# Five buffers for the upper and four for the lower halves of the expert weights in place of three each, and nine load buffers in place of twelve

## The chip, the cores and the metric

The kernel runs on one core of a Trainium2 chip. The metric is the device time of one launch in microseconds (us), the median of several executions. TensorE is called PE here, VectorE DVE, ScalarE ACT, SyncE SP, as in the profile; SP issues the transfers from memory.

## The reference

Two decoder layers over 256 tokens of width 1024, all in fp32. Nearly all of the time goes into the last step, the routed experts: a router picks two of eight experts for each token, and each expert is a SwiGLU of width 3584.

```
xt = rmsnorm(x) * (1 + scale) + shift                  # 256 x 1024
logits = xt @ w_router                                 # 8 experts
top_logits, top_idx = top_k(logits, 2); gates = softmax(top_logits)
y_e = (silu(x_e @ w_gate[e]) * (x_e @ w_up[e])) @ w_down[e]    # rows x_e routed to e
x = x + gate * sum over the chosen experts of gates * y_e
```

Ahead of it stand layer 0 (a retention mixer and a dense SwiGLU of width 2816) and layer 1's pooling mixer; behind it the last norm.

## The kernel before, in words

**Weights.** Every weight is read once, in parts of 128 x 2048 fp32 (1 MB). `load` (L126) takes a buffer from the deque `ring` and issues one transfer on SP's queue. That queue is in order: a load that waits for its buffer holds up all loads behind it. `weights` (L136) then splits the part: ACT writes the upper half `w_hi` (the value rounded to the matmul type fp32r), DVE the lower half `w_lo` = raw − `w_hi`, both at L113 in `split`. `w_hi` and `w_lo` have `N_SPL` = 3 buffers each, so the split of a part can begin once PE is through with the part three before it. The loads of the expert stage rotate over 12 lasting buffers: six `raw`, four `e8`, and the two old tiles `cb` and `T_l`, which are free by then (`SPARE`, L59, whose first number is the place in the deque).

**Matmuls.** A wide expert (ranks 1 to 3 by the number of tokens) takes three matmuls per 512 weight columns in `mm3` (L156 to L158: upper x upper, lower weight x upper, upper weight x lower token). A narrow one has the upper and lower halves of 64 tokens side by side and needs two, `mm2` (L738 with `w_hi`, L739 with `w_lo`).

**Blocks.** Each expert has seven blocks. A block has two parts of gate weights, two of up and two of down; the down parts come two blocks later. That makes 336 parts, numbered 0 to 335 in this document, from about 460 us to about 1358 us. The first seven blocks are those of a narrow expert; then blocks come in the order wide, narrow, wide, narrow, wide, narrow, narrow, repeated.

**Small work between the parts.** `g_out` and `u_out` (L766) take a narrow block's results out of the banks, L774 transposes and adds them, `sg` (L753) and `moe_h` (L755) do a wide block's. `behind_next` ties these evictions behind a split of the coming weights. Where an expert's tokens are gathered, `prepare` runs 32 small matmuls (L720), eight evictions `xe_f` on ACT (L240), and a split into `xe_n` (L113). Where an expert ends, `combine` scales two banks into `y_g` (DVE, L799), splits them into `yp` (L113), multiplies back (L809, L810) and adds into `xs` (DVE, L811). Eight blocks from the end `f_row` (ACT, L193) is made for the last norm.

**Order.** A scheduler fixes one static order on each engine when the program is built, from the code and the buffers. An instruction that waits holds up all behind it on its engine.

Of the kernel before, what the change touches and what calls it, by code (L numbers as in the profile page):

```python
# [11 lines left out]
R = mybir.dt.float32r  # L12
# [33 lines left out]
N_RAW, N_SPL, N_E8, N_OHT = 6, 3, 4, 4  # L46
# [9 lines left out]
assert len(set(BLOCKS)) == NE * NJ and BLOCKS[-1] == (NE - 1, NJ - 1)  # L56
ALWAYS = math.inf

SPARE = ((8, "a8", 2, 2), (11, "kd", 1, 3), (12, "qk", 1, 10), (12, "cb", 1, ALWAYS), (9, "T_l", 1, ALWAYS))  # L59

ADA_B, ADA_O, ADA_F = (1, 1, 1, 1, 1, 1, 1, 1), (3, 3, 0, 0), (0, 0, 4, 4, 3, 3, 3, 3, 3, 3, 0)

# [2 lines left out]
def trunk(ctx, tc, x, cols, c_row, const, ada_0, ada, w_0, w_in, w_out, f_gu, f_dn, pool_w, m_g, m_u, m_d, out):  # L65
# [13 lines left out]
    def buf(tag, shape, bufs=1, dt=F, name=None):  # L79
        return act.tile([P] + shape, dt, tag=tag, name=name or tag, bufs=bufs)  # L80
# [24 lines left out]
    cb = buf("cb", [2048])[:, :D]  # L105
# [6 lines left out]
    def split(hi, lo, src):  # L112
        return nc.scalar.activation(hi, src, AF.Copy), nc.vector.tensor_sub(lo, src, hi.bitcast(F))  # L113

    @contextmanager
    def behind(*instructions):

        with ExitStack() as s:
            for i in instructions:
                s.enter_context(tc.issue_after(i.ins))  # L120
            yield


    ring = deque([("raw", N_RAW, ALWAYS)] * N_RAW)

    def load(src, in_halves=False):  # L126
        tag, bufs, uses = ring.popleft()
        if uses > 1:
            ring.append((tag, bufs, uses - 1))
        t = buf(tag, [2048], bufs, name="raw")  # L130
        n = 1024 if in_halves else 2048
        for c in range(0, 2048, n):
            nc.sync.dma_start(t[:, c:c + n], src[:, c:c + n])
        return t

    def weights(src, step=2048, held=((), (), (), ()), in_halves=False):  # L136

        parts, splits = [], []
        for h in range(0, src.shape[1], 2048):
            t = load(src[:, h:h + 2048], in_halves)  # L140
            hi = buf("w_hi", [2048], N_SPL, R)
            lo = buf("w_lo", [2048], N_SPL, R)
            for c in range(0, 2048, step):
                strip = slice(c, c + step)
                with behind(*held[len(splits)]):
                    splits.append(split(hi[:, strip], lo[:, strip], t[:, strip]))
            parts.append((hi, lo))

        def at(c, n=512):
            hi, lo = parts[c // 2048]  # L150
            return hi[:, c % 2048:c % 2048 + n], lo[:, c % 2048:c % 2048 + n]
        at.splits = splits
        return at
# [119 lines left out]
    for k in range(KD):  # L273
        ada_sums(ada_0[k], (k, 8 + k), None if k else ada_first)
        nc.scalar.activation(mod[:, k:k + 1], mod[:, k:k + 1], AF.Identity, bias=col[:, C_ADAB + k:C_ADAB + k + 1])
        nc.vector.scalar_tensor_tensor(a1[:, k:k + 1], mod[:, 8 + k:9 + k], scale1[:, k:k + 1], gain_of(0, 0)[:, k:k + 1],
                                       op0=ALU.add, op1=ALU.mult)
        h_k = mod_T(hh[:, k], hl[:, k], xT[:, k], a1, mod, k)
        at = weights(w_0[k], 1024, held=((), h_k))
        for f in range(4):  # L280
            wh, wl = at(512 * f)
            for b in range(TB):
                mm3(first[f][b], hh[:, k, tok(b)], hl[:, k, tok(b)], wh, wl, k == 0, k == KD - 1)
    kd = buf("kd", [K_BAND - K_DM])
# [85 lines left out]
    for i, f in enumerate(W_REST):  # L370
        at = weights(w_in[i])
        pss = [bank() for _ in range(TB)]
        for k in range(KD):
            wh, wl = at(512 * k)
            for b in range(TB):
                mm3(pss[b], hh[:, k, tok(b)], hl[:, k, tok(b)], wh, wl, k == 0, k == KD - 1)
        win_done(f, pss, st)
        for fn, h in after.get(i, []):
            fn(h, st)
        ada_next(ADA_B[i])  # L380
    g_row = row(buf("g_row", [D]), mcol(0, 2))
    acc = [[bank() for _ in range(2)] for _ in range(TB)]
    for h in range(NH):
        yT = st[f"yT{h}"]
        at = weights(w_out[h])
        last = h == NH - 1
        steps = [(i, b) for i in range(4) for b in range(TB)]
        if last:
            steps = [(i, b) for b in range(TB) for i in range(4)]
        for i, b in steps:  # L390
            for n in range(2):
                wh, wl = at(1024 * i + 512 * n)
                mm3(acc[b][n], yT[:, 0, i, tok(b)], yT[:, 1, i, tok(b)], wh, wl, h == 0 and i == 0, last and i == 3)
        ada_next(ADA_O[h])
# [205 lines left out]
    srcs = sources()  # L600


    once = [ring[i][:2] + (1,) for i in range(2)]
    ring.rotate(-2)
    for place, *spare in SPARE:
        ring.insert(place, tuple(spare))
# [416 lines left out]
```

## Time and profile before

| | |
|---|---|
| Median of 3 runs | 1374.83 us (1373.33 to 1375.98) |
| The profiled execution | 1376.74 us, of which its span 1375.0 us |
| PE matmul, DVE, ACT busy | 96 %, 88 %, 71 % of the span |
| Mean granted TensorE clock | 0.991 |
| Moved from memory | 475 MB, 346 GB/s over the span |

The busy shares are averages over all stages. In the profile's groups a line such as L113 stands for every split, so the tile's name tells which one it is. An idle time in brackets is the engine's wait just before the row, with the instruction that released it. A row of PE is longer than the distance to the next row, since matmuls overlap.

### The profile page before, as it was taken

What the parts mean: (1) busy time and instruction counts of PE and PEld (TensorE: products, weight loads), DVE (VectorE), ACT (ScalarE), POOL (GpSimd) and SP (SyncE); (2) the same over time, 40 slices, a digit from 0 to 9 for tenths busy, and PEclk for the clock granted to TensorE, in tenths of its full rate; (3) what the DMA queues carried; (4) which work ended last, traced back from release to release, by engine and by line L of the source; (5) the groups of instructions that cost most, each with busy time, mean ns of one, the idle gap of its engine ahead of it and who ended that gap; (6) DMA issues with size and microseconds to landing.
All of it is one profiled execution on the core that took longest, in us unless ns stands there. A gap on an engine that the chain in (4) does not pass through costs nothing.

```text
span 1375.0 us, 16794 instructions
## 1 busy us (share of the span) xinstructions
PE 1315.1 (96%) x6136; PEld 1052.5 (77%) x6136; DVE 1215.2 (88%) x1121; ACT 978.2 (71%) x942; POOL 0.2 (0%) x4
## 2 busy tenths in 40 slices
PE   7999998999999899999999999999999999999995
PEld 5787876888887777778778877788778777777874
DVE  7889867998867698999989999989998989999997
ACT  6655465444445698878878887878878878788884
POOL 0000000000000000000000000000000000000000
PEclk9999999999999899999999999999999999999998
DMA  9987885998786599999999999999999999999960
GB/s 384 380 278 260 324 287 207 338 378 362 297 333 238 209 427 344 369 364 424 419 377 401 424 334 334 412 356 426 412 357 409 360 334 401 404 367 418 424 279 33
DMA packets 66474, 477.30 MB, mean 347 GB/s; under 512 B 7377, under 2 KB 7761, under 8 KB 8658
## 3 DMA queue, kind: packets, MB, share of 16 engines
q1 hardware_dynamic: 66386, 476.17, 88.3%
q8 instruction: 50, 0.82, 0.2%
q14 instruction: 38, 0.31, 0.1%
HBM read 475.10 MB, written 1.05 MB: 346 GB/s over the span
## 4 chain that ended last, share of the span: by engine, by line
PE 70%; DVE 16%; ACT 6%; issue 4%; DMA 3%; DVEq 0%; SPq 0%; ACTq 0%
PE bank L157 15%; PE bank L158 15%; PE bank L156 14%; DVE w_lo L113 12%; PE bank L739 8%; PE bank L738 7%; PE tbank L774 3%; ACT w_hi L113 3%; DMA raw<-in_m_d_dram 2%; PE tbank L720 2%; PE tbank L250 1%; DVE raw L167 1%; ACT xe_f L240 1%; DMA raw<-in_m_u_dram 1%; DVE dT L113 1%
## 5 line engine op out<-in xcount | busy, mean ns | idle before, releaser
L113 DVE TENSOR_TENSOR w_lo<-raw,w_hi 128x2048 fp32r<-128x2048 f32 (+1 forms) x413 | 907.1, 2225 | 82.5 <-ACT w_hi L113 78.4
L113 ACT ACTIVATE w_hi<-raw 128x2048 fp32r<-128x2048 f32 (+1 forms) x413 | 763.8, 1868 | 199.1 <-PE bank L158 142.3
L739 PE MATMUL bank<-w_lo,xe_n 128*128 128x512 f32 x560 | 230.7, 412 | 12.7 <-DVE w_lo L113 9.6
L738 PE MATMUL bank<-w_hi,xe_n 128*128 128x512 f32 x560 | 221.1, 396 | 2.0 <-DVE xe_n L113 2.0
L739 PEld LDWEIGHTS bank<-w_lo,xe_n 128*128 128x128 f32 x560 | 105.8, 189 | 57.5 <-DVE w_lo L113 38.0
L156 PE MATMUL bank<-w_hi,T_h 128*128 128x512 f32 x352 | 140.9, 401 | 3.0 <-ACT T_h L113 3.0
L157 PE MATMUL bank<-w_lo,T_h 128*128 128x512 f32 x352 | 138.5, 393 | 2.4 <-DVE w_lo L113 2.4
L158 PE MATMUL bank<-w_hi,T_l 128*128 128x512 f32 x352 | 138.8, 394 | 1.7 <-DVE T_l L113 1.7
L157 PE MATMUL bank<-w_lo,xe 128*128 128x512 f32 x336 | 132.5, 394 | 0.9 <-DVE w_lo L113 0.9
L156 PE MATMUL bank<-w_hi,xe 128*128 128x512 f32 x336 | 131.6, 392 | 0.0
L158 PE MATMUL bank<-w_hi,xe 128*128 128x512 f32 x336 | 130.9, 390 | 0.0
L738 PEld LDWEIGHTS bank<-w_hi,xe_n 128*128 128x128 f32 x560 | 106.0, 189 | 22.1 <-DVE xe_n L113 2.1
L167 DVE SCALAR_TENSOR_TENSOR raw<-raw,cb 128x1024 f32<-128x1024 f32 x96 | 114.4, 1218 | 1.7 <-DMA raw<-in_ada_dram 1.7
L739 PE MATMUL bank<-w_lo,dT 128*128 128x512 f32 x280 | 104.4, 411 | 7.2 <-DVE w_lo L113 6.7
L738 PE MATMUL bank<-w_hi,dT 128*128 128x512 f32 x280 | 100.1, 394 | 1.7 <-DVE dT L113 1.7
L157 PE MATMUL bank<-w_lo,dT 128*128 128x512 f32 x256 | 100.8, 394 | 0.7 <-DVE w_lo L113 0.7
L158 PE MATMUL bank<-w_hi,dT 128*128 128x512 f32 x256 | 99.8, 390 | 0.0
L156 PE MATMUL bank<-w_hi,dT 128*128 128x512 f32 x256 | 94.2, 389 | 0.0
L156 PEld LDWEIGHTS bank<-w_hi,T_h 128*128 128x128 f32 x352 | 66.6, 189 | 17.7 <-ACT T_h L113 4.3
L158 PEld LDWEIGHTS bank<-w_hi,T_l 128*128 128x128 f32 x352 | 66.5, 189 | 17.1 <-DVE T_l L113 3.2
L157 PEld LDWEIGHTS bank<-w_lo,T_h 128*128 128x128 f32 x352 | 66.6, 189 | 16.4 <-DVE w_lo L113 2.8
L157 PEld LDWEIGHTS bank<-w_lo,xe 128*128 128x128 f32 x336 | 63.1, 188 | 16.3 <-DVE w_lo L113 3.8
(227 smaller groups left out, 1430.5 us busy)
## 6 DMA issues: line engine op xcount, KB each, us to landing
raw<-in_m_g_dram SPq DMA_DIRECT2D x112, 1024.0 KB, 7.5
raw<-in_m_u_dram SPq DMA_DIRECT2D x112, 1024.0 KB, 7.6
raw<-in_m_d_dram SPq DMA_DIRECT2D x112, 1024.0 KB, 7.3
raw<-in_ada_dram SPq DMA_DIRECT2D x48, 1024.0 KB, 7.2
raw<-in_f_gu_dram SPq DMA_DIRECT2D x22, 1024.0 KB, 6.9
raw<-in_w_in_dram SPq DMA_DIRECT2D x16, 1024.0 KB, 5.2
raw<-in_f_dn_dram SPq DMA_DIRECT2D x11, 1024.0 KB, 7.2
raw<-in_w_dram SPq DMA_DIRECT2D x8, 1024.0 KB, 8.7
```

The source lines that it names most:

```text
L113: return nc.scalar.activation(hi, src, AF.Copy), nc.vector.tensor_sub(lo, src, hi.bitcast(F))
L156: nc.tensor.matmul(ps, xh, wh, start=start, stop=False)
L157: nc.tensor.matmul(ps, xh, wl, start=False, stop=False)
L158: nc.tensor.matmul(ps, xl, wh, start=False, stop=stop)
L167: nc.vector.scalar_tensor_tensor(s, s, 1.0, cb, op0=ALU.mult, op1=ALU.mult, accum_out=mod[:, m:m + 1])
L240: nc.scalar.activation(out, ps, AF.Identity, scale=a[:, k:k + 1], bias=s[:, k:k + 1])
L250: nc.tensor.transpose(ps[:, i * P:(i + 1) * P], src[:, i * P:(i + 1) * P], ident)
L720: nc.tensor.matmul(ps[:, i * ns:(i + 1) * ns], xn[:, b, c], oh[:, b, 0:ns], start=(b == 0), stop=(b == TB - 1))
L738: nc.tensor.matmul(ps, x, wh, start=start, stop=False)
L739: nc.tensor.matmul(ps, x, wl, start=False, stop=stop)
L774: nc.tensor.matmul(ps[:, i, c], a[:, c * P:(c + 1) * P], fold, start=True, stop=True)
```

## The change

Before the expert stage begins, two deques of split buffers grow. `uppers` gets the two old tiles `cb` and `T_l` beside the three `w_hi`, `lowers` one buffer of tag `e8` beside the three `w_lo`. `SPARE` loses its entries for `cb` and `T_l`, and `ring` one `e8`, so that nine lasting buffers stay for loads. The four slots of tag `e8` still rotate among all who ask for the tag, loads and lower halves alike.

```
-SPARE = ((8, "a8", 2, 2), (11, "kd", 1, 3), (12, "qk", 1, 10), (12, "cb", 1, ALWAYS), (9, "T_l", 1, ALWAYS))
+SPARE = ((8, "a8", 2, 2), (11, "kd", 1, 3), (12, "qk", 1, 10),)
...
     ring = deque([("raw", N_RAW, ALWAYS)] * N_RAW)
+    uppers, lowers = deque([("w_hi", N_SPL)] * N_SPL), deque([("w_lo", N_SPL)] * N_SPL)
...
             t = load(src[:, h:h + 2048], in_halves)
-            hi = buf("w_hi", [2048], N_SPL, R)
-            lo = buf("w_lo", [2048], N_SPL, R)
+            (tag_hi, n_hi), (tag_lo, n_lo) = uppers[0], lowers[0]
+            uppers.rotate(-1)
+            lowers.rotate(-1)
+            hi = buf(tag_hi, [2048], n_hi, R, name="w_hi")
+            lo = buf(tag_lo, [2048], n_lo, R, name="w_lo")
...
+    uppers.extend([("cb", 1), ("T_l", 1)])
+    lowers.append(("e8", N_E8))
+    ring.remove(("e8", N_E8, ALWAYS))
     once = [ring[i][:2] + (1,) for i in range(2)]
```

The lines after `weights` move by four, those of the expert stage by seven. The scheduler gives the three engines that feed PE another order at some places; three of them follow.

ACT at the gather for a narrow expert, at parts 92 (`w_hi_5290`) and 93 (`w_hi_5296`); `w_hi_5322` is part 94. Before:

```order
L766 ACTIVATE u_out_5254<-bank_5237 128x512
L113 ACTIVATE w_hi_5290<-raw_5288 128x2048
L113 ACTIVATE w_hi_5296<-raw_5294 128x2048
L240 ACTIVATE xe_f_5261<-tbank_5260,mod_93,acol13_2980 128x64 x8
L732 ACTIVATE ohT_5256<-tbank_5316 128x256
L113 ACTIVATE xe_n_3387<-xe_f_5261 128x8x64
L113 ACTIVATE w_hi_5322<-raw_5320 128x2048
```

The same place in the changed kernel:

```order
L773 ACTIVATE u_out_5254<-bank_5237 128x512
L244 ACTIVATE xe_f_5261<-tbank_5260,mod_93,acol13_2980 128x64 x8
L113 ACTIVATE w_hi_5290<-raw_5288 128x2048
L113 ACTIVATE xe_n_3387<-xe_f_5261 128x8x64
L113 ACTIVATE w_hi_5296<-raw_5294 128x2048
L739 ACTIVATE ohT_5256<-tbank_5316 128x256
L113 ACTIVATE w_hi_5322<-raw_5320 128x2048
```

The two upper halves have moved from ahead of the eight evictions `xe_f` to behind them. At the gather of part 32 the order changes in the same way, and at the gather of part 165 one upper half moves so.

DVE where the first wide expert is combined; the lower halves are those of parts 139 (`w_lo_6242`), 140 (`6281`), 141 (`6287`), 142 (`6330`) and 143 (`6336`). Before:

```order
L755 TENSOR_TENSOR moe_h_6272<-bank_6245,sg_6270 128x512
L811 SCALAR_TENSOR_TENSOR xs_72<-tbank_6274,gate_p_3536,xs_72 128x512
L113 TENSOR_TENSOR w_lo_6281<-raw_6278,w_hi_6280 128x2048
L799 TENSOR_TENSOR y_g_6315<-bank_4580,g2_row_3496 128x512
L113 TENSOR_TENSOR w_lo_6287<-raw_6284,w_hi_6286 128x2048
L113 TENSOR_TENSOR yp_6314<-y_g_6315,yp_6314 128x512
L799 TENSOR_TENSOR y_g_6319<-bank_4581,g2_row_3496 128x512
L811 SCALAR_TENSOR_TENSOR xs_72<-tbank_6323,gate_p_3536,xs_72 128x512
L113 TENSOR_TENSOR w_lo_6330<-raw_6327,w_hi_6329 128x2048
L113 TENSOR_TENSOR yp_6314<-y_g_6319,yp_6314 128x512
L113 TENSOR_TENSOR w_lo_6336<-raw_6333,w_hi_6335 128x2048
```

The same place in the changed kernel:

```order
L762 TENSOR_TENSOR moe_h_6272<-bank_6245,sg_6270 128x512
L818 SCALAR_TENSOR_TENSOR xs_72<-tbank_6274,gate_p_3536,xs_72 128x512
L806 TENSOR_TENSOR y_g_6315<-bank_4580,g2_row_3496 128x512
L806 TENSOR_TENSOR y_g_6319<-bank_4581,g2_row_3496 128x512
L113 TENSOR_TENSOR yp_6314<-y_g_6315,yp_6314 128x512
L818 SCALAR_TENSOR_TENSOR xs_72<-tbank_6323,gate_p_3536,xs_72 128x512
L113 TENSOR_TENSOR w_lo_6281<-raw_6278,w_hi_6280 128x2048
L113 TENSOR_TENSOR yp_6314<-y_g_6319,yp_6314 128x512
L113 TENSOR_TENSOR w_lo_6287<-raw_6284,w_hi_6286 128x2048
L113 TENSOR_TENSOR w_lo_6330<-raw_6327,w_hi_6329 128x2048
L113 TENSOR_TENSOR w_lo_6336<-raw_6333,w_hi_6335 128x2048
```

Both `y_g`, the first `yp` and an `xs` have moved ahead of the lower half of part 140. At `f_row` (part 284) ACT's order changes likewise: both `f_row` evictions now stand ahead of the upper half of part 284, where it stood between them.

SP's queue with the counters that each load waits for (`DVE_49` is a count of DVE's, `PE_49` one of PE's); `raw_6278` is the load of part 140. Before:

```order
L133 DMA raw_6233<-in_m_d_dram 128x2048 [waits DMAHW4_49,DVE_49]
L133 ISA
L133 DMA raw_6239<-in_m_d_dram 128x2048 [waits DMAHW5_49,DVE_49]
L133 ISA
L133 DMA raw_6278<-in_m_g_dram 128x2048 [waits DMAHW6_49,DVE_49]
```

The same place in the changed kernel:

```order
L134 DMA raw_6233<-in_m_d_dram 128x2048 [waits DMAHW4_49,DVE_49]
L134 ISA
L134 DMA raw_6239<-in_m_d_dram 128x2048 [waits DMAHW5_49,DVE_49]
L134 ISA
L134 DMA raw_6278<-in_m_g_dram 128x2048 [waits DMAHW6_49,DVE_49,PE_49]
```

The load of part 140 now also waits for PE: its `e8` slot held the lower half of part 135, which PE reads. Over the stage 41 loads wait for PE in this way, and before none. Nineteen of them follow closely behind what they wait for: nine loads wait for PE to finish the part five before them (140 is one), ten for the part six before.

## Rows read from the trace of the kernel before

**Rows 1.** The page: busy time, share, instructions; last chain by engine
```profile
PE 1315.1 (96%) x6136; PEld 1052.5 (77%) x6136; DVE 1215.2 (88%) x1121; ACT 978.2 (71%) x942; POOL 0.2 (0%) x4
...
PE 70%; DVE 16%; ACT 6%; issue 4%; DMA 3%; DVEq 0%; SPq 0%; ACTq 0%
```

**Rows 2.** Windows: length, PE, PEld, DVE, ACT, POOL busy, clock, DMA share, GB/s
```profile
600.00:800.00 200.00, 197.91 (x947) 160.55 (x946) 187.76 (x114) 166.38 (x135) 0.00 (x0) 1.00 0.99 400
...
sum 890.00, PE 865.69 PEld 694.72 DVE 832.20 ACT 735.73 POOL 0.00; mean PE 173.14 PEld 138.94 DVE 166.44 ACT 147.15 POOL 0.00
```

**Rows 3.** Groups, 460 to 1350: busy, mean ns, idle before and its releaser
```profile
L113 DVE TENSOR_TENSOR w_lo<-raw,w_hi 128x2048 fp32r<-128x2048 f32 x331 | 745.3, 2287 | 42.2 <-ACT w_hi L113 38.4
L113 ACT ACTIVATE w_hi<-raw 128x2048 fp32r<-128x2048 f32 x333 | 631.5, 1919 | 104.4 <-PE bank L158 59.2 <-PE bank L738 20.7 <-DMA raw<-in_m_d_dram 7.6
...
L739 PEld LDWEIGHTS bank<-w_lo,xe_n 128*128 128x128 f32 x559 | 105.4, 189 | 57.5 <-DVE w_lo L113 38.0
```

**Rows 4.** Waits, 460 to 1350: us in total, times, longest
```profile
PEld bank L739 <- DVE w_lo L113: 57.4, 99, 1.9
...
PE bank L739 <- DVE w_lo L113: 16.3, 29, 1.4
```

**Rows 5.** Timeline of ACT, 690 to 722: start, length, group, idle before
```profile
692.86 3.72 ACT L113 ACTIVATE w_hi<-raw 128x2048 fp32r<-128x2048 f32 x2
699.58 2.47 ACT L240 ACTIVATE xe_f<-tbank,mod,acol 128x64 f32<-128x64 f32 x8 [3.00 <-PE tbank L720]
...
702.16 0.68 ACT L113 ACTIVATE xe_n<-xe_f 128x512 fp32r<-128x512 f32 x1
```

**Rows 6.** Timeline of DVE, 690 to 712
```profile
704.68 4.49 DVE L113 TENSOR_TENSOR w_lo<-raw,w_hi 128x2048 fp32r<-128x2048 f32 x2 [1.12 <-ACT w_hi L113]
```

**Rows 7.** Timeline of PE, 694 to 709
```profile
695.86 3.68 PE L720 MATMUL tbank<-oh,xn_m 128*128 128x64 f32 x32
...
700.50 0.49 PE L156 MATMUL bank<-w_hi,xe 128*128 128x512 f32 x1
...
706.08 1.00 PE L774 MATMUL tbank<-fold,g_out 128*128 128x64 f32 x8
...
707.78 0.48 PE L156 MATMUL bank<-w_hi,xe 128*128 128x512 f32 x1
```

**Rows 8.** Timeline of ACT, 534 to 545
```profile
541.81 2.48 ACT L240 ACTIVATE xe_f<-tbank,mod,acol 128x64 f32<-128x64 f32 x8 [3.00 <-PE tbank L720]
```

**Rows 9.** Timeline of ACT, 892 to 906
```profile
896.37 2.47 ACT L240 ACTIVATE xe_f<-tbank,mod,acol 128x64 f32<-128x64 f32 x8 [2.51 <-PE tbank L720]
```

**Rows 10.** Timeline of DVE, 822 to 850
```profile
830.63 0.69 DVE L799 TENSOR_TENSOR y_g<-bank,g_row 128x512 f32<-128x512 f32 x1 [0.18 <-PE bank L158]
...
833.44 0.69 DVE L113 TENSOR_TENSOR yp<-y_g,yp 128x512 fp32r<-128x512 f32 x1
...
834.96 0.75 DVE L811 SCALAR_TENSOR_TENSOR xs<-tbank,gate_p,xs 128x512 f32<-128x512 f32 x1 [0.23 <-PE tbank L810]
...
838.43 2.29 DVE L113 TENSOR_TENSOR w_lo<-raw,w_hi 128x2048 fp32r<-128x2048 f32 x1
```

**Rows 11.** Timeline of ACT, 1219 to 1230
```profile
1223.46 0.60 ACT L193 ACTIVATE f_row<-tbank 128x512 f32<-128x512 f32 x1 [0.73 <-PE tbank L187]
```

**Rows 12.** Timeline of DVE, 1219 to 1230
```profile
1225.90 4.49 DVE L113 TENSOR_TENSOR w_lo<-raw,w_hi 128x2048 fp32r<-128x2048 f32 x2 [0.85 <-ACT w_hi L113]
```

**Rows 13.** Timeline of ACT, 424 to 446
```profile
436.56 0.63 ACT L218 ACTIVATE xn_m<-xs 128x512 f32<-128x512 f32 x1 [1.08 <-DVE xs L546]
```

**Rows 14.** Waits of SP's queue, whole span: us in total, times, longest
```profile
SPq L133 <- DVE w_lo L113: 759.8, 309, 27.5
```

**Rows 15.** Loads of L133, 600 to 1300, issue to landing
```profile
DMA to landing us min/median/max: 4.7/7.4/10.2
```

**Rows 16.** Timeline of PE, 818.6 to 820.2
```profile
819.32 0.39 PE L158 MATMUL bank<-w_hi,xe 128*128 128x512 f32 x1
```

**Rows 17.** Timeline of ACT, 822 to 846
```profile
825.46 1.92 ACT L113 ACTIVATE w_hi<-raw 128x2048 fp32r<-128x2048 f32 x1 [0.32 <-ACT sg L753]
```

## The prediction

> **What bounds the kernel now.** I read the page first: PE is busy 96% of the span, and the chain that ended last lies 70% on PE and 16% on DVE [rows 1]. Then the windows of the expert stage: from 460 to 1350 us PE is busy 865.69 of 890 us and DVE 832.20, and in the calmest stretch PE stands still for only 2.1 us of 200, with the transfers at 0.99 of the engines' time [rows 2]. So PE, DVE and the transfers run close together, and PE is ahead by a little. The groups say why: a lower half costs DVE 2.29 us and an upper half costs ACT 1.92 [rows 3], while PE spends 2.79 us on a wide part (two parts from 700.50 to 706.08, [rows 7]). Next, the waits: PE's weight loads wait for `w_lo` 57.4 us in 99 pieces, but its matmuls only 16.3 [rows 4]; the first hide mostly under the matmul still running. That sets a ceiling for any gain from deeper buffers: PE's whole idle time in the stage is 890 − 865.69 = 24.3 us, and the weight loads that wait for `w_lo` in the narrow gate and up parts have 38.0 [rows 3]. Last, ACT's waits before `w_hi`: 104.4 us, of which 79.9 for PE to give a split buffer back [rows 3]. Those are what five and four buffers take away; ACT is not the bound, so the 79.9 is no gain by itself.
>
> **The change part by part.** No instruction is added or removed in the expert stage: the same 336 parts are loaded, split and multiplied. What changes is who waits, and the order.
>
> *The added buffers.* They let `w_hi` run four or five parts ahead of PE and `w_lo` four, where it was three. But `g_out`, `u_out` and `sg` on ACT, `moe_h` and `y_g` on DVE still wait for a PE result of a part three back and stand in order before the next split, so the new lead is lost there about once a block. I therefore take a part of the waits only: half of the 16.3 us for which PE's matmuls wait for a lower half [rows 4], −8. Bounds: 0, if the lead is lost everywhere, and −38.0, if all waits of that group go.
>
> *The gather at part 92.* Before, the two upper halves of 92 and 93 were done by 696.58, ahead of the eight `xe_f` at 699.58, which waited 3.00 us for PE's gather [rows 5]. PE's gather itself (695.86, 3.68 long, [rows 7]) does not move. Now ACT waits idle for it with the two splits behind it: `xe_f` ends at 702.05, then the upper half of 92 to 703.97, its lower half on DVE at 2.25 us apiece [rows 6] to 706.3, the lower halves' `xe_n` of 0.69, the lower half of 93 to 709.3, and part 93 on PE takes 2.79 more, to 712.0. L774's 1.7 us, which stood between 93 and 94, goes ahead of 92 meanwhile and is hidden. Part 94 began at 707.78 [rows 7]: +4.3. The gather at part 32 shows the same eight evictions with the same 3.00 us ahead of them [rows 8] and the same new order: +4.3. At part 165 only one upper half moves behind `xe_f` (896.37, [rows 9]): it would be split from 898.7 to 900.7, its lower half to 902.9, PE done with it at 905.7, about when the next part can begin; between 0 and 2.1, I take +1.0. Behind each of the waiting `xe_f` stand the uppers of the next parts, then DVE's lowers for the same parts, then PE.
>
> *The combine at part 140.* DVE's first `y_g` started at 830.63 [rows 10] when PE had its banks ready. From there, by the new order: second `y_g` to 831.9, `yp` (0.69) to 832.6 behind ACT's half of it, `xs` (0.75) to 833.8, and only then the lower half of 140 to 836.1, `yp`, and three more lower halves at 2.25, to 843.4. Before, the lower half of 143 ended at 838.43 + 2.29 = 840.7. So +2.7 in DVE's row, which PE feels in full if it has no lead there: 0 to 2.7, and I take 2.7, since DVE runs without gaps around it.
>
> *`f_row` at part 284.* The second `f_row` ends at 1224.06 [rows 11], and now the upper halves of 284 and 285 both follow it: 1226.0 and 1227.9, so the lower half of 285 ends at about 1230.4. Before it was the first of the pair from 1225.90 [rows 12], done at 1228.2: +2.2.
>
> *The start.* In the router's chain just before the stage ACT and DVE get two uppers and one lower more among the small steps, 2 x 1.92 + 2.29 = 6.1 at most and 0 at least. ACT has gaps there, as 1.08 us before `xn_m` [rows 13], and the splits are work done early: +1.5. In the first blocks two uppers stand ahead of one that PE needs sooner: 0 to 3.8, again +1.5.
>
> *The loads.* Before, SP's queue waited for the DVE, 309 times and 759.8 us [rows 14], which says that loads are issued as buffers come free. Nine buffers and the shared `e8` slots make 19 loads wait for PE to be through with a part five or six before. For part 140 I can put the room from rows: part 135 ended on PE at 819.32 + 0.39 [rows 16], the upper half of 140 began at 825.46 [rows 17], so 5.7 us, and the fastest load lands after 4.7, the median one after 7.4 [rows 15]. A load issued into a nearly empty queue should be near the fastest. What waits behind such a load are all later loads, then `w_hi`, `w_lo` and PE. Price 0 if all land as the fastest one, 9 x (7.4 − 5.7) = 15 us at the median, and I take +1, since the loads behind the gate do not need to land sooner than one part apart.
>
> The Trainium skill's page "SBUF — State Buffer" ("The DMA setup-cost knee") speaks against this change: it puts a fixed cost of about 2 us on each transfer, whatever its size. By it a 1 MB load alone takes an estimated 4.4 us, which the trace's 4.7 agrees with, and a queue that runs empty at each of 19 gates would lose up to 19 x 2 = 38 us; whether that shows depends on the slack.
>
> *The sum.* 4.3 + 4.3 + 1.0 + 2.7 + 2.2 = 14.5 from the order, 1.5 + 1.5 + 1.0 = 4.0 from start and loads, −8 from the waits: +10.5. On the profiled execution's 1376.74 that makes 1387.2; this execution lies 1.9 above the median of the runs, so I predict 1385.3 us.
>
> **The rivals.** *A, faster.* The run-ahead is real, and the buffers carry DVE over the narrow blocks, where its 2.29 us per part exceed PE's. For it: 99 waits of PE's weight loads for `w_lo` and ACT's 79.9 us of waiting for PE. Against it: `moe_h` and `y_g` in order on DVE. It decides from a gain of 18.5 us, the costs above; at 30, between that and the ceiling of 38.0, the time is 1376.7 + 18.5 − 30 − 1.9 = 1363.3.
>
> *B, no change in effect.* The leads are pinned, and the moved splits lie in stretches where PE has slack that absorbs them within a block or two, so that gains and costs are both near nothing: 1375, within 0.2% (2.75 us), which is what a measurement of this kernel can tell from none. For it: all but about five places of the order are alike. Against it: PE stands still 2.1 us in 200, so there is little slack to absorb with.
>
> *C, loads late.* The gates bind: at the nine close ones the load takes 7.4 us instead of 4.7, 9 x 2.7 = 24 more: about 1409. For it: the transfers were at 0.99 busy and nine buffers hold less ahead than twelve. Against it: a load into an empty queue shares with nobody.
>
> **How the numbers follow.** My forecast 0.55, with a range of its own of 1378 to 1395 (by the bounds of its terms: without part 165, the start and the loads and with a gain of 14 it is +2 or so, with the start's and loads' upper ends +20). A 0.23, B 0.15, C 0.07. The range 1364 to 1400 leaves out about half of A and most of C, under 2 in 10. Faster by over 0.2%: A and a little of my own case, 0.24; within: B and the low end of mine, 0.15; slower: 0.61.
>
> **What would show it.** In the profile after: at the gather of part 92 ACT idle for some 6 us before `xe_f` with no `w_hi` after `u_out`, and PE waiting 3 to 4 us for `w_hi` or `w_lo` of 92 and 93; on DVE the two `y_g` side by side before a lower half, and PE's next waits there; ACT's waits for PE before `w_hi` well below 79.9; PE's matmul waits for `w_lo` near 8 outside those places; loads' waits for DVE turned into some for PE, without `w_hi` waiting for a load more than before. I would be wrong if PE's wait for `w_lo` fell by 20 us or more, if PE did not wait at part 92, or if `w_hi` waited for loads for tens of us.

## The result: 37 us slower, and the profile after

The changed kernel took 1411.53 us (median of 4, 1408.49 to 1414.85) against 1374.08 us for the one before: a ratio of 1.0267, 95% interval 1.0252 to 1.0283. That is 36.7 us slower. The direction was forecast; the time lies 11.5 us above the stated range, and the 10.5 us that the sum gave are less than a third of it.

The page of the changed kernel, busy line and the last chain by engine, to be read against [rows 1]:

```profile
PE 1330.0 (94%) x6136; PEld 1066.4 (76%) x6136; DVE 1212.3 (86%) x1121; ACT 967.4 (69%) x942; POOL 0.2 (0%) x4
...
PE 36%; DVE 11%; DMA 6%; ACT 5%; issue 5%; SPq 0%; DVEq 0%; ACTq 0%
```

PE's share fell from 96% to 94% of a span that is 32.7 us longer, though it has the same 6136 matmuls to do. Its busy time rose by 14.9 us all the same: the same matmuls took longer, and the granted clock fits that. The windows of the changed kernel, with the columns of [rows 2]:

```profile
460.00:600.00 140.00, 130.41 (x589) 105.48 (x590) 112.39 (x89) 105.68 (x100) 0.00 (x0) 0.90 0.73 286
600.00:800.00 200.00, 192.20 (x900) 154.84 (x899) 180.60 (x110) 157.10 (x125) 0.00 (x0) 0.98 0.93 387
...
sum 890.00, PE 850.85 PEld 685.11 DVE 797.04 ACT 693.41 POOL 0.00; mean PE 170.17 PEld 137.02 DVE 159.41 ACT 138.68 POOL 0.00
```

The first of these windows in the kernel before:

```profile
460.00:600.00 140.00, 133.99 (x660) 107.87 (x659) 128.47 (x93) 120.25 (x110) 0.00 (x0) 0.99 0.91 360
```

The granted clock of the stretch from 460 to 600 us is 0.90 of full speed, where it was 0.99, and PE gets through 589 records instead of 660. From 600 to 800 it is 0.98 instead of 1.00. Over the whole execution the mean fell from 0.991 to 0.978; 1407.7 x 0.022 − 1375.0 x 0.009 = 18.6 us more of full speed were withheld (not all of it is lost time, since PE was idle in part of it). The prediction had no term for that.

The waits of the changed kernel from 460 to 1350, against [rows 3] and [rows 4]:

```profile
ACT g_out L773 <- PE bank L746: 52.6, 23, 4.9
PEld bank L746 <- DVE w_lo L113: 49.5, 72, 2.1
ACT dT L113 <- DVE h_n L785: 46.9, 22, 5.4
...
PE bank L746 <- DVE w_lo L113: 19.9, 29, 1.8
ACT w_hi L113 <- PE bank L745: 16.9, 12, 4.3
...
ACT w_hi L113 <- DMA raw<-in_m_u_dram: 13.4, 21, 2.0
```

Two of these groups in the kernel before:

```profile
ACT g_out L766 <- PE bank L739: 8.1, 14, 1.3
...
ACT dT L113 <- DVE h_n L778: 3.3, 3, 1.9
```

ACT's waits for PE before `w_hi`, 79.9 us before, are down to 16.9 in the largest of their groups. But PE's waits for a lower half are where they were: 49.5 and 19.9 after 57.4 and 16.3. ACT's idle time has moved instead: it now waits 52.6 us for PE before `g_out` (8.1 before) and 46.9 us for DVE before `dT` (3.3 before). So ACT got ahead with the splits and then stood at the next eviction, which is where the prediction said that the new lead would be lost; PE got nothing from it. ACT's waits for loads before `w_hi` rose too, from 14.1 to 24.0 us over their three groups, which the prediction had not expected.

Where the time is lost shows when the end of the last matmul of each part is taken from both traces and subtracted. This is a selection; at a stall itself, single parts are up to 4 us later than those behind it (parts 32 and 8 show that).

```
part                     0     8    16    20    30    32    36    46    90    96   110   122   130   146   188   266   282   286   334
lag of after, us       1.2   6.0   2.4   9.6   7.8  18.5  15.6  15.5  14.4  21.0  20.9  23.2  23.3  26.3  27.1  28.3  28.5  32.7  33.4
```

Between the places the lag stands still to some tenths of a microsecond over dozens of parts. This is no rate that changed, but a handful of stalls: 15.5 us up to part 46, in two steps of about 7 (by part 30) and 8 (parts 31 to 36), and then about 7, 2, 3 and 4 at parts 92 to 96, 120 to 122, 140 to 144 and 284 to 286.

**Part 92**, to be read against [rows 5] to [rows 7]. ACT:

```profile
706.78 0.59 ACT L773 ACTIVATE u_out<-bank 128x512 f32<-128x512 f32 x1
713.97 2.48 ACT L244 ACTIVATE xe_f<-tbank,mod,acol 128x64 f32<-128x64 f32 x8 [6.58 <-PE tbank L727]
716.29 1.95 ACT L113 ACTIVATE w_hi<-raw 128x2048 fp32r<-128x2048 f32 x1
```

DVE:

```profile
718.28 2.29 DVE L113 TENSOR_TENSOR w_lo<-raw,w_hi 128x2048 fp32r<-128x2048 f32 x1 [8.14 <-ACT w_hi L113]
```

PE (rows at which it waited, and its gather):

```profile
710.25 3.68 PE L727 MATMUL tbank<-oh,xn_m 128*128 128x64 f32 x32
...
716.50 1.10 PE L781 MATMUL tbank<-fold,g_out 128*128 128x64 f32 x8 [1.37 <-ACT xe_f L244]
...
720.62 0.79 PE L161 MATMUL bank<-w_lo,xe 128*128 128x512 f32 x1 [1.83 <-DVE w_lo L113]
```

Clock and busy times there (columns of [rows 2]):

```profile
716.00:720.00 4.00, 2.29 (x17) 1.99 (x17) 1.72 (x1) 4.00 (x5) 0.00 (x0) 0.99 1.01 426
720.00:727.00 7.00, 6.38 (x15) 4.99 (x16) 7.00 (x5) 6.50 (x6) 0.00 (x0) 0.52 1.01 427
727.00:740.00 13.00, 13.00 (x59) 10.67 (x58) 11.27 (x9) 10.16 (x7) 0.00 (x0) 1.00 0.57 221
```

ACT stands idle for 6.58 us in front of `xe_f` with nothing done behind `u_out`, DVE then for 8.14 us, and PE for 1.37 and 1.83, as the steps of the prediction had it. The lag grows by 6.6 us here, where the prediction had 4.3. Behind the stall PE's clock is at its lower level (0.52 over 7 us, 1.2 instead of 2.4 GHz for nearly all of it), which the prediction did not have.

**Parts 140 and 284**, on DVE, against [rows 10] and [rows 12]:

```profile
854.18 1.37 DVE L806 TENSOR_TENSOR y_g<-bank,g_row 128x512 f32<-128x512 f32 x2 [2.79 <-PE bank L162]
...
857.52 2.28 DVE L113 TENSOR_TENSOR w_lo<-raw,w_hi 128x2048 fp32r<-128x2048 f32 x1
...
860.32 6.69 DVE L113 TENSOR_TENSOR w_lo<-raw,w_hi 128x2048 fp32r<-128x2048 f32 x3
```

```profile
1254.43 8.90 DVE L113 TENSOR_TENSOR w_lo<-raw,w_hi 128x2048 fp32r<-128x2048 f32 x4 [3.98 <-ACT w_hi L113]
```

At part 140 the kernel before had, ahead of the first `y_g` and right behind it, the lower halves of 140 and 141:

```profile
828.16 2.28 DVE L113 TENSOR_TENSOR w_lo<-raw,w_hi 128x2048 fp32r<-128x2048 f32 x1
...
831.24 2.28 DVE L113 TENSOR_TENSOR w_lo<-raw,w_hi 128x2048 fp32r<-128x2048 f32 x1
```

Now both `y_g` run side by side, and part 140's lower half starts 3.34 us behind the first of them, where it was done before it. At 284 DVE stands idle 3.98 us, not 0.85.

**The start.** The clearest change is at the load queue. The windows of the changed kernel, and then of the kernel before:

```profile
460.00:480.00 20.00, 19.27 (x88) 16.05 (x88) 13.29 (x26) 15.61 (x13) 0.00 (x0) 0.90 0.43 158
480.00:500.00 20.00, 19.11 (x87) 15.74 (x88) 19.69 (x13) 13.76 (x12) 0.00 (x0) 0.91 0.82 309
```

```profile
460.00:480.00 20.00, 20.00 (x96) 16.43 (x95) 16.55 (x19) 17.09 (x15) 0.00 (x0) 0.95 0.61 225
480.00:500.00 20.00, 18.84 (x90) 14.78 (x89) 19.85 (x12) 18.47 (x15) 0.00 (x0) 1.00 1.01 427
```

In the changed kernel the transfers are busy 0.43 and 0.82 of these stretches, before 0.61 and 1.01. SP's queue, from 425 to 600 us, now has this group of waits:

```profile
SPq L134 <- PE bank L746: 22.9, 7, 7.7
```

Part 8's load is the first of those that share their slot with a lower half (the programs have 42 of them, not 41): it waits for PE to finish part 3, and that is when PE has only just begun the stage. In the trace it is issued at 469.4 us, as PE ends part 3, and lands at 477.0, 1.9 us before ACT splits it; before the change it lay ready for 56.7 us. The load of part 20 waits for part 15 in the same way and lands 1.7 us before its split, where it had 24.4. Part 8's upper half then comes too late, and this row of PE waits for it:

```profile
480.84 1.09 PE L745 MATMUL bank<-w_hi,xe_n 128*128 128x512 f32 x2 [1.56 <-ACT w_hi L113]
```

**Part 32**, against [rows 8]. Here the loads aren't late: those of 31 and 32 land 10.2 and 13.4 us before their splits. ACT's order has the upper half of 33 ahead of 31's, and 32's behind `xe_f`. PE waits for a lower half, ACT stands idle, and the clock over the whole stretch is 0.73:

```profile
546.99 0.73 PE L746 MATMUL bank<-w_lo,dT 128*128 128x512 f32 x2 [1.59 <-DVE w_lo L113]
```

```profile
553.00 2.48 ACT L244 ACTIVATE xe_f<-tbank,mod,acol 128x64 f32<-128x64 f32 x8 [6.11 <-PE tbank L727]
555.33 1.95 ACT L113 ACTIVATE w_hi<-raw 128x2048 fp32r<-128x2048 f32 x1
```

```profile
540.00:560.00 20.00, 17.76 (x81) 15.01 (x80) 6.90 (x8) 13.31 (x18) 0.00 (x0) 0.73 0.60 236
```

### The profile page after: what moved, and what is told of

Same layout as the page of the kernel before. It is cut to its first block, busy times and chain, and to the rows that moved or that the text cites. A ratio compares the mean times of both kernels' runs of the same rounds, so it can differ in the third digit from the quotient of the medians.

```text
span 1407.7 us, 16939 instructions
## 1 busy us (share of the span) xinstructions
PE 1330.0 (94%) x6136; PEld 1066.4 (76%) x6136; DVE 1212.3 (86%) x1121; ACT 967.4 (69%) x942; POOL 0.2 (0%) x4
## 4 chain that ended last, share of the span: by engine, by line
PE 36%; DVE 11%; DMA 6%; ACT 5%; issue 5%; SPq 0%; DVEq 0%; ACTq 0%
DVE w_lo L113 10%; PE bank L161 7%; PE bank L162 7%; PE bank L160 7%; PE bank L746 6%; PE bank L745 5%; ACT w_hi L113 3%; DMA raw<-in_m_u_dram 3%; DMA raw<-in_m_d_dram 3%; PE tbank L781 2%; PE tbank L727 2%; ACT xe_f L244 1%; DVE xs L818 0%; ACT dT L113 0%; PE tbank L254 0%
## 5 line engine op out<-in xcount | busy, mean ns | idle before, releaser
L745 PE MATMUL bank<-w_hi,xe_n 128*128 128x512 f32 x560 | 227.3, 407 | 6.3 <-ACT w_hi L113 4.3
L746 PEld LDWEIGHTS bank<-w_lo,xe_n 128*128 128x128 f32 x560 | 109.5, 195 | 50.8 <-DVE w_lo L113 29.7
L745 PEld LDWEIGHTS bank<-w_hi,xe_n 128*128 128x128 f32 x560 | 109.5, 196 | 28.6 <-ACT w_hi L113 5.8
L162 PEld LDWEIGHTS bank<-w_hi,T_l 128*128 128x128 f32 x352 | 66.8, 190 | 16.9 <-DVE T_l L113 3.0
```

What stands on the lines that cost most here:

```text
L162: nc.tensor.matmul(ps, xl, wh, start=False, stop=stop)
L745: nc.tensor.matmul(ps, x, wh, start=start, stop=False)
L746: nc.tensor.matmul(ps, x, wl, start=False, stop=stop)
```

## The experiments

Theory O: the loss comes from the places where the order on ACT and DVE changed, each stall made longer by a stretch at the lower clock. Theory L: it comes from loads that are late, because there are fewer buffers for them or because they wait for PE. All ratios are to the kernel before on the same chip, with 95% intervals.

### Nine load buffers alone

```
-    uppers.extend([("cb", 1), ("T_l", 1)])
-    lowers.append(("e8", N_E8))
```

> Only the loss of three load buffers: nine for loads, but three split buffers of each kind as before, so no load waits for PE, and the order on ACT and DVE is that of before but for the first combine (parts 49 to 62). Theory O (the loss comes from the places where the order of ACT and DVE changed, each stall followed by a stretch at the lower TensorE clock): within 3 us of before. Theory L (loads come late, because nine buffers hold less ahead and because loads wait for PE): if the number of buffers matters, 10 us or more slower; if only the waits for PE matter, no change.

Measured: 1376.05 us against 1375.01, ratio 1.0004 (0.9994 to 1.0013). Three load buffers less cost nothing that can be measured; the half of theory L that names the number of buffers falls.

### Upper halves alone, lower halves alone

`e2_upper_only` drops the lines that append `e8` to `lowers` and remove it from `ring`. `e3_lower_only` drops the line that extends `uppers` and puts `cb` and `T_l` back into `SPARE`.

> Five buffers for the upper halves and three for the lower, ten for loads, none of which waits for PE. The order differs from before up to part 63 and is the same behind it. Theory O: only a part of the loss up to part 46 (17 us in the changed kernel), some 3 to 10 us slower, and nothing behind part 63. Theory L: no change, since no load waits for PE. If the longer run-ahead of ACT had a gain of its own (the 8 us of the prediction), it would show here as a lag that shrinks behind part 63.

> Four buffers for the lower halves (the fourth from the tag e8, with its 53 loads that wait for PE, 19 of them for a part five or six before) and three for the upper, eleven for loads. The order at the gather of part 92, at the combine of part 140 and at f_row is as before; at the gather of part 165 both upper halves now stand behind xe_f, and part 8 comes late. Theory O: 5 to 10 us slower, lost at the start and at part 165, each with a stretch at the lower clock. Theory L: the waits for PE cost as in the changed kernel, 15 to 35 us slower, spread over the stage.

Measured: the upper halves alone 1373.66 us, ratio 0.9983 (0.9970 to 0.9995), a little faster, where theory O had 3 to 10 us slower; the lower halves alone 1403.52 us, ratio 1.0213 (1.0186 to 1.0241), 29 us slower. The second was far from the 5 to 10 us that I expected by theory O, and inside what L expected. But the loss isn't spread evenly: about 7 us of the lag come in the first 40 parts, and about 16 are added at parts 86, 98, 110, 122, 266 and 278, each two parts behind a place where the order now puts `dT` on ACT ahead of an upper half that it followed before (84, 96, 108, 120, 264, 276), and at 166 to 168, since both upper halves of 164 and 165 now stand behind `xe_f`. The expectation had left those swaps of `dT` out. The changed kernel has two of them, at 120 and 264. The one at 120 is its step of 2 us at part 122, which the prediction's sum doesn't have: ACT waits 1.90 us for `h_n` before `dT`, while the load of 120 landed 3.3 us before its split. At part 165 PE stands as it did at part 92 in the changed kernel:

```profile
916.61 0.79 PE L161 MATMUL bank<-w_lo,xe 128*128 128x512 f32 x1 [1.83 <-DVE w_lo L113]
```

### The same four lower buffers without a shared slot

Against `e3_lower_only`, `T_l` also leaves `SPARE`, and the fourth `e8` goes back to the loads:

```
-    lowers.append(("e8", N_E8))
-    ring.remove(("e8", N_E8, ALWAYS))
+    lowers.append(("T_l", 1))
```

(`cb` stays with the loads, so eleven load buffers as in `e3_lower_only`.)

> Four buffers for the lower halves as in e3_lower_only, but the fourth is the tile T_l, used by nobody else, so no load waits for PE; eleven buffers for loads (six raw, four e8, cb). The order is that of before but for one place. If the 28 us of e3_lower_only come from the slots of e8 that loads and lower halves share (through the loads' waits for PE or through the order that the scheduler makes of them), within 3 us of before; if a fourth lower half itself disturbs, 15 us or more slower.

Measured: 1375.07 us against 1373.96, ratio 1.0006 (0.9996 to 1.0015). A fourth lower buffer is harmless; the 29 us come from the slots that loads and lower halves share, be it by the waits or by the order.

### Shared slots with the order tied back

The slots act in two ways: a load really waits, and the scheduler, which sees that dependence when it makes the order, puts other work first. `e7_late` has all the buffers of the change from block 9 on; `e4_late_pinned` has the same and ties the order back, first the eight `xe_f` of a narrow gather, then the two `y_g`, then the halves of `f_row`:

```
+            if late:
+                with behind(coming.splits[1][0]):
+                    late.pop()()
+                    step()
...
+            for n in range(2):
+                with behind(*coming.splits[n]) if p == 1 else nullcontext():
+                    steps.pop(0)()
...
+                with behind(at_gate[h][0]):
```

> All the buffers of the change (five, four, nine), but the split buffers join only from block 9 on (part 56), and the order at four places is tied back to that of before: the xe_f of the narrow gathers behind the second upper half, the two y_g of the combine at part 140 one by one behind the lower halves of 140 and 141, f_row behind the upper halves of 284 and 285. 33 loads still wait for PE, 15 of them for a part five or six before. Theory O: within 4 us of before, the rest at part 122. Theory L: 12 us or more slower, since the buffers and the waits of the loads are those of the changed kernel from part 56 on.

> The buffers of e4_late_pinned, joining at block 9 too, but without the order tied back. The loads and their waits for PE are the same as in e4_late_pinned. Theory O: the lags of the changed kernel at parts 92 (5.7), 122 (2.3), 140 (2.8) and 284 (4.5) and their stretches at the lower clock, so 14 to 19 us slower than before. Theory L: the time of e4_late_pinned, 3.5 us slower than before.

Measured: 1378.53 us, ratio 1.0031 (1.0020 to 1.0042), with the order tied; 1390.37 us, ratio 1.0126 (1.0109 to 1.0143), without. The loads are the same in both; 13 us lie in the order of the four tied places (by the lags, at 92, 140 and 284; at 165 none is lost). In `e4_late_pinned` the loads of 600 to 1300 us took

```profile
DMA to landing us min/median/max: 4.8/13.1/19.7
```

from issue to landing, nearly twice the median of [rows 15], and 33 of them wait for PE, and still the kernel loses no more than 4.3 us, most of it at part 122 (3.9 us of lag between parts 110 and 122), which wasn't tied. Of the 15 loads that follow closely, 12 land only 0.1 to 0.3 us before their split, so ACT takes them as they come, and PE's lag moves by 1.2 us at most at any of them. Long landings are then no measure of loss: a load that is issued in a row behind others has to queue. By the fixed cost of about 2 us per transfer that the Trainium skill's page "SBUF — State Buffer" ("The DMA setup-cost knee") states, 15 close waits that each emptied the queue would cost 30 us, an estimate. The 4.3 us of this run leave no room for that in PE's time.

### One place alone, and the clock

`e5_moved92` is the kernel before with one thing moved; `e6_moved92_filled` adds matmuls that nobody reads:

```
-        coming = None if src is None else weights(src)
+        source += 1
+        late = ((evicted[-1],), (evicted[-1],)) if source == 46 else ((), (), (), ())
+        coming = None if src is None else weights(src, held=late)
...
+            if i == 15:
+                ps, xw = tbank(), ready[BLOCKS[16][0]][0]
+                for k in range(14):
+                    nc.tensor.matmul(ps, xw[:, 0, 0], xw[:, 0, 0:4].rearrange("p k t -> p (k t)"), start=True, stop=True)
```

> The kernel before with one thing changed: at part 92 the upper halves of 92 and 93 stand behind the eight xe_f on ACT, as in the changed kernel; all buffers as before, and the rest of the order too. Theory O: PE stands still for some 4 us at parts 92 and 93, TensorE's granted clock falls to its lower level behind that, and the lag stays to the end: 4.3 us by the stall alone, 5 to 8 us with the stretch at the lower clock. Theory L: without late loads nothing to lose, within 2 us of before.

> As e5_moved92, with 14 matmuls of 128x512 whose result nobody reads in PE's order behind part 91, where PE would stand still. They take about 3.2 us, less than the stall. If the lower clock behind the stall costs time of its own, its stretch vanishes and the lag at part 100 is 1 to 3 us less than in e5_moved92; if the clock is only a sign, the two kernels take the same time within 1 us.

Measured: 1383.49 us against 1373.96, ratio 1.0059 (1.0045 to 1.0072), 8.1 us by the ratio (the medians lie 9.5 apart); with the fill 1378.98 us, ratio 1.0031 (1.0016 to 1.0045), 4.3 us. The windows of `e5_moved92` around the place:

```profile
690.00:704.00 14.00, 10.97 (x70) 8.88 (x68) 5.88 (x5) 7.40 (x13) 0.00 (x0) 1.00 0.69 293
704.00:711.00 7.00, 6.32 (x15) 4.98 (x16) 5.63 (x4) 3.92 (x4) 0.00 (x0) 0.51 0.75 253
```

and of `e6_moved92_filled`:

```profile
690.00:704.00 14.00, 13.45 (x80) 11.17 (x78) 5.87 (x5) 7.41 (x13) 0.00 (x0) 1.00 0.72 301
704.00:711.00 7.00, 6.76 (x35) 5.59 (x34) 7.00 (x5) 5.39 (x6) 0.00 (x0) 1.00 0.69 225
```

Two splits on the wrong side of eight evictions cost 8.1 us in a kernel whose buffers are untouched; in the profiled execution the lag grows by 6.5 us at this place, as it does in the changed kernel (6.6). Without the fill PE is busy 10.97 of 14 us and its clock then is 0.51; with it 13.45 of 14, and the clock stays at 1.00. Doing useless work saved 3.8 us by the ratios (the two intervals only just touch) and 2.9 us by the lags (3.6 in place of 6.5). What is left, 4.3 us (2.2 to 6.2) or 3.6, agrees with the stall alone that the prediction had worked out, 4.3 us.

### The start

`e9_pinned` is the changed kernel with the ties of `e4_late_pinned`; `e10_upper_first` lets the fourth lower buffer join only at block 9.

> The changed kernel with the four ties of e4_late_pinned, but with the split buffers from the start of the stage, as in the changed kernel. Theory O: the lag of the first 46 parts stays (17 us in the changed kernel), the lags at parts 92, 140 and 284 go, so 17 to 22 us slower than before; of the changed kernel's 37 us the ties give back some 14 to 18. Theory L: as slow as the changed kernel.

> As e9_pinned, but the fourth lower buffer, with its slot shared with loads, joins only at block 9; the two more for the upper halves are there from the start. If the shared slot makes the loss at the start (part 8's load waits for PE to finish part 3, and the order puts part 8 behind part 11, 23 and 24 ahead of 20), the time falls to that of e4_late_pinned within 4 us: 0 to 8 us slower than before. If the upper halves' earlier splits among the router's small steps make it, it stays 15 us or more slower.

Measured: 1399.12 us against 1374.91, ratio 1.0173 (1.0156 to 1.0190), 24 us slower and so 2 more than theory O's upper end; and 1379.15 us, ratio 1.0028 (1.0018 to 1.0038). The window 460 to 600 of the one and of the other:

```profile
460.00:600.00 140.00, 128.61 (x586) 105.07 (x586) 111.39 (x92) 103.67 (x99) 0.00 (x0) 0.89 0.73 285
```

```profile
460.00:600.00 140.00, 134.21 (x662) 109.69 (x662) 130.75 (x111) 116.51 (x110) 0.00 (x0) 0.97 0.88 343
```

The shared slot in the first nine blocks costs 20 us, and the early upper halves among the router's steps nearly nothing. The traces split the 20 by place. Up to part 30, where `e9_pinned` lags 8 us behind `e10_upper_first`, loads are late in earnest: those of parts 8 and 20 land 2.2 and 3.3 us before their splits, so theory L holds there, through the wait for PE and not through the number of buffers. Between parts 31 and 46 the lag of `e9_pinned` against `e10_upper_first` grows from 8 to 17 us, though the load of part 32 lands 12.4 us before its split: there it is the order (33 ahead of 31, and 32 behind the first of the `xe_f`), which the tie behind the upper half of 33 doesn't reach. No run takes the two apart, for the order at part 32 comes from the shared slot too.

### Deeper split buffers with nothing shared

`e11_four_four` gives `cb` to the upper halves, `T_l` to the lower and leaves all four `e8` to the loads:

```
-    uppers.extend([("cb", 1), ("T_l", 1)])
-    lowers.append(("e8", N_E8))
-    ring.remove(("e8", N_E8, ALWAYS))
+    uppers.append(("cb", 1))
+    lowers.append(("T_l", 1))
```

`e12_upper_from_block_9` gives both tiles to the upper halves, from block 9 on.

> Four buffers for the upper halves (the fourth is cb) and four for the lower (the fourth is T_l), ten for loads; nothing is shared, no load waits for PE, and the order is that of before behind part 63. Theory O: no loss behind part 63; a gain of at most 2 to 3 us as in e2_upper_only, or none. If deeper split buffers have the gain of the prediction when nothing speaks against them, 6 us or more faster.

> Five buffers for the upper halves from block 9 on, three for the lower, ten for loads. The order on ACT and DVE is that of before but for the first combine. The run-ahead of the upper halves by itself, without what it moves at the start: by e2_upper_only, whose lag shrinks by 1 to 2 us behind part 63, 0 to 3 us faster.

Measured: 1368.97 us against 1374.91, ratio 0.9959 (0.9945 to 0.9973), 5.6 us faster than before, between the two expectations; and 1372.19 us, ratio 0.9979 (0.9970 to 0.9988), 2.9 us faster. `e11_four_four` beats both kernels. Its waits from 460 to 1350:

```profile
PEld bank L745 <- DVE w_lo L113: 50.6, 78, 1.9
...
ACT w_hi L113 <- PE bank L162: 23.1, 34, 2.0
...
PE bank L745 <- DVE w_lo L113: 17.5, 27, 1.5
```

and its first window:

```profile
460.00:600.00 140.00, 136.93 (x685) 111.82 (x685) 131.47 (x86) 125.01 (x114) 0.00 (x0) 1.00 0.94 368
```

PE's waits for lower halves are those of before, 50.6 and 17.5, so the gain isn't where the prediction looked for it. By 600 us PE has 685 records where the kernel before had 660: most of the gain lies in the first seven blocks, which are all narrow. What exactly shrinks there was not tested.

## Why the prediction was wrong

**Right: the places and the mechanism.** The gathers at 32 and 92, the combine at 140 and `f_row` at 284 lose time as their steps said; rival B, that the order's moves cost nothing, falls with `e5_moved92`. The stall at 92 was sized 4.3 us and measured 4.3 by the ratio, 3.6 by the lag, once the clock was kept up. At part 140 the lag grows by 3.0 us, for which the sum had 2.7.

**Wrong: the price of a stall.** Each was costed as the time for which PE stands still. Behind it PE ran at its lower clock: 8.1 us at part 92 in place of 4.3. By the lags of the changed kernel part 92 cost 6.6, part 32 7.8 (4.3 in the sum), part 284 4.2 (2.2 in the sum); that the clock makes the difference was tested at 92 alone. At part 165, for which the sum had 1.0, nothing is lost. The ties give back 13 us, with the buffers late (1.0126 less 1.0031) as with the changed kernel itself (1.0267 less 1.0173), for which the sum had 4.3 + 1.0 + 2.7 + 2.2 = 10.2. Part 122 stood nowhere in it.

**Wrong: the start and the loads, the step that failed most.** The sum had 1.5 for the router's chain, 1.5 for the first blocks, 1.0 for all loads and 4.3 for part 32, together 8.3 us; `e9_pinned` less `e10_upper_first` shows 20, and the lag of the changed kernel at part 46 is 15.5. The loads' term was worked out at part 140 [rows 16, 17], where PE is far into its work and the room was 5.7 us. The first of those gates, part 8's, stands where PE has only begun, and its load landed 1.9 us before its split. The place that decides was not the one whose rows were read.

**Wrong: the gain.** −8 was set against the costs. Split buffers can give 5.6 us, when nothing is shared (`e11_four_four`, with four and four); with shared slots and the order tied, the kernel is 4.3 us slower than before. In the changed kernel none of the gain is to be seen: PE's matmuls wait 19.9 us for a lower half in the narrow blocks, not 8.

**The rivals.** C named the loads and came near in time (1409), but by luck: it priced nine close gates of the whole stage at 2.7 us, and behind part 56 those cost at most 4.3 us together, while the start, which it didn't name, costs 20. A's gain of 30 us was never there; it was also more than the 24.3 us for which PE stands idle in the stage, which the prediction itself had named as a ceiling.

Going from the changed kernel to the one before in steps, 13 us go with the order of four places, 20 with the shared slot at the start and 4 with the rest (`e10_upper_first`, 3.8). Each step is the difference of two runs, so they make the measured 37 by construction; what speaks for the division is that the 13 came out twice, from two pairs of kernels.

## What to carry to other kernels

A buffer that is lent to a second user out of a rotating set ties both users together at every turn, and the scheduler makes its order around that tie: give the second user a slot of its own. When a change moves an instruction that waits ahead of work that feeds the bound engine, look for every such move and not for the largest alone, price the stall and the slower clock behind it, and read the gate nearest to the start of a stage first, since there the engine that it waits for has no lead. Where buffers are added, look at whether the waits of the bound engine fall; shorter waits of the others aren't a gain.

## What the hardware showed that was not expected

Two idle times of PE close together, 1.37 and 1.83 us, in a kernel otherwise at full clock, were followed by about 7 us at half the clock, in the changed kernel and, with 1.35 and 1.83 us, in `e5_moved92` (0.52 and 0.51); 14 matmuls without a use kept the clock at 1.00 and saved 3.8 us by the ratios, 2.9 by the lags.
